# Remainder parts of MLP weights: every second half piece by an accumulating DMA, conversions three half pieces ahead

## The chip, the cores and the metric

The kernel runs on one core of a Trainium2 chip. The metric is device time in microseconds of one execution. The kernel before takes 2416.2 us (median of 2 runs, 2415.84 to 2416.57).

## The reference, cut to what matters

A decoder trunk of two layers for 256 tokens of width 2048, in float32. Each layer has a token mixer and then an MLP, both behind an RMSNorm and added to the residual stream. The mixer of layer 0 is latent attention (MLA), that of layer 1 a Mamba-2 scan (SSM).

```python
def squared_relu_mlp(h, w_in, w_out):
    u = jax.nn.relu(h @ w_in)
    return (u * u) @ w_out

for i in range(DEPTH):
    h = rms_norm(x, mix_norm_g[i])
    x = x + (mla_mixer(h, ...) if i % 2 == 0 else ssm_mixer(h, ...))
    h = rms_norm(x, mlp_norm_g[i])
    x = x + squared_relu_mlp(h, mlp_w_in[i], mlp_w_out[i])
```

`w_in` is [2048, 8192] and `w_out` is [8192, 2048], so each MLP reads 128 MB of float32 weights, and both of them 256 MB of the 452 MB that the whole kernel moves.

## The kernel before, in words

**Products.** The tokens are the stationary operand (two tiles of 128), the weights stream through TensorE 512 columns at a time. A float32 product is taken as three passes over operands that are split into a rounded part H (type float32r) and the exact remainder L = raw - H: for each 128 rows of weights and each token tile `block` issues H.H (L227), H.L (L228) and L.H (L229), where the second factor is the weights'. So the weights' H is needed by the first matmul and their L by the second.

**Pieces and half pieces.** A weight piece is [128, 4 x 512] float32, 1 MB. `Flow` holds the list of all pieces in the order of use (`sequence`, which puts MLA first, then MLP 0, SSM, MLP 1). Each MLP has 64 pieces of `w_in` (keys "mi") and 64 of `w_out` (keys "mo"). A piece is converted in two half pieces of [128, 1024]. The second element of a half's record, `k`, is the first of its four row blocks: 0 in the first half of a piece, 2 in the second.

- `load` takes one of three raw buffers (`wr`) and puts a 1 MB DMA on SyncE's queue (L75). A buffer is free again when both halves of its piece have been converted.
- `convert` takes one buffer each of the pools `wh` and `wl` (three of 4 KB per partition in each), lets ScalarE copy the half piece into `wh` with rounding (L101) and VectorE subtract: `wl` = raw - `wh` (L102).
- `piece` hands the halves out. Before it hands out half `j` it asks for the load of pieces up to three ahead, and for the conversion of halves up to `j + 2` (`ahead` is (3, 2)).

With three buffers, half `j + 2` goes into the buffers that half `j - 1` leaves. ScalarE's copy for `j + 2` therefore waits until TensorE has finished half `j - 1`, and there are then two half pieces of TensorE time before `j + 2` is wanted.

**Order.** The order on TensorE is that of the program text. A planner with costs of its own orders the instructions of the other engines and of the DMA queues, and sets all waits. Each engine and each queue takes its instructions in that order: an instruction that waits holds up those behind it.

**In the MLP.** A `w_in` block (four pieces) ends in a Relu (L384) and a Square (L385) on ScalarE for each token tile. Then come four transposes on TensorE and a split (L203 on ScalarE, L204 on VectorE), again for each tile. A `w_out` block (four pieces) ends in an addition to the residual on VectorE (L307). After four blocks of the one kind come four of the other, four times in each MLP. GpSimd has nothing to do in the MLP but three small instructions of the norm between two parts (L194, L299, L300).

**Gain rows.** `gain_tile` (L272) loads rows of gains, 256 KB each, on SyncE's queue into the pool `gb` of three buffers. They are read at the ends of MLA, MLP 0 and SSM (L284), and in the SSM at L914 and L948.

Of the kernel before, what the change touches and what calls it, by code (L numbers as in the profile page):

```python
"""MLA / Mamba-2 decoder trunk (2 layers, 256 tokens) for one NeuronCore.

Layout: tokens are the stationary operand of every large product (two tiles of
128), the weights stream through as the moving operand, 512 columns at a time.
Large float32 products run as three float32r passes over operands split into a
rounded part H and the exact remainder L (H.H + H.L + L.H).
RMSNorm's per-token factor is applied where a product leaves PSUM.  The scan has
one chunk of 256 tokens that starts from the zero state, so its output is the
intra-chunk term.
"""  # L10
# [2 lines left out]

# [10 lines left out]
AF = mybir.ActivationFunctionType  # L24
ALU = mybir.AluOpType
AX = mybir.AxisListType
PSUM = bass.MemoryType.PSUM
# [29 lines left out]


class Flow:
    """Weight pieces in the order of use: loaded, split into H and L, handed out."""  # L60

    def __init__(self, nc, pools, seq, ahead):
        self.nc, self.pools, self.seq, self.ahead = nc, pools, seq, ahead
# [17 lines left out]
    def convert(self, upto):  # L81
        while self.done < min(upto, len(self.halves)):
            j = self.done
            i, k, nk, n = self.halves[j]
            self.load(i + 1)
            raw = self.raw[i][:, k * n:(k + nk) * n]
            h = self.pools["wh"].tile([P, 1024], F32R, tag="wh", name=f"wh{j}")
            lo = self.pools["wl"].tile([P, 1024], F32R, tag="wl", name=f"wl{j}")
            if n == 64:
                for q, t in enumerate((h, lo)):  # L90
                    v = t.rearrange("p (k r n) -> p k r n", r=2, n=64)
                    w = raw.rearrange("p (k n) -> p k n", n=64)[:, 8 * q:8 * q + 8]
                    self.nc.scalar.activation(v[:, :, 0], w, AF.Copy)
                    self.nc.vector.tensor_tensor(v[:, :, 1], w, v[:, :, 0].bitcast(F32), ALU.subtract)
                self.split[j] = (h, lo)
                self.done += 1
                continue
            w = 512 if j == 0 else nk * n
            for o in range(0, nk * n, w):
                v = slice(o, o + w)  # L100
                self.last = self.nc.scalar.activation(h[:, v], raw[:, v], AF.Copy)  # L101
                self.nc.vector.tensor_tensor(lo[:, v], raw[:, v], h[:, v].bitcast(F32), ALU.subtract)  # L102
            self.split[j] = (h, lo)
            self.done += 1

    def piece(self, key):
        """Yields (first k tile, H, L) with H, L as [128, k tiles, columns]."""
        i = self.seq_at
        assert self.seq[i][0] == key, (self.seq[i][0], key)
        self.seq_at += 1  # L110
        while self.used < len(self.halves) and self.halves[self.used][0] == i:
            j = self.used
            self.load(i + self.ahead[0])
            self.convert(j + 1 + self.ahead[1])
            _, k, nk, n = self.halves[j]
            h, lo = self.split.pop(j)
            if n == 64:
                self.used += 1
                yield [t.rearrange("p (k n) -> p k n", n=P) for t in (h, lo)]
                return  # L120
            yield (k, nk, h[:, :nk * n].rearrange("p (k n) -> p k n", k=nk),
                   lo[:, :nk * n].rearrange("p (k n) -> p k n", k=nk))
            self.used += 1
# [4 lines left out]
class Trunk:  # L128
    def __init__(self, tc, ctx, d, out):
        self.tc, self.nc, self.d, self.out = tc, tc.nc, d, out  # L130
        nc = self.nc
        pool = lambda name, bufs, **kw: ctx.enter_context(tc.tile_pool(name=name, bufs=bufs, **kw))
        self.c = pool("const", 1)
        self.st = pool("stat", 24)
        self.res = pool("res", 1)
        self.xtp = pool("xt", 8)
        self.k4 = pool("k4", 8)
        self.s2 = pool("s2", 8)
        self.gb = pool("gb", 3)
        self.wp = {"raw": pool("raw", 3), "wh": pool("wh", 3), "wl": pool("wl", 3)}  # L140
        self.acc = pool("acc", 4, space=PSUM)
        self.sm = pool("sm", 2, space=PSUM)
        self.yp = pool("yp", 2, space=PSUM)
        self.queue, self.pump = [], None
        self.nsm = 0
        self.uid = 0

# [1 line left out]
    def name(self, s):  # L149
        self.uid += 1  # L150
        return f"{s}_{self.uid}"
# [35 lines left out]
        return pool.tile([P, 4, 256], dt, tag=pool.name, name=self.name(pool.name))  # L187

    def rsqrt(self, ssq, n, width, eps=EPS, scale=None):
        """(ssq / width + eps) ** -0.5, per token"""  # L190
        nc = self.nc
        v, r = self.stat(n), self.stat(n)
        nc.vector.tensor_scalar(v, ssq, 1.0 / width, eps, ALU.mult, ALU.add)  # L193
        nc.gpsimd.tensor_tensor(r, v, self.mhalf[:, :n], ALU.pow)  # L194
        return r
# [8 lines left out]
        self.nc.vector.tensor_tensor(lo, src, h.bitcast(F32), ALU.subtract)  # L204

    def transposes(self, src, h, lo, t, wide=True):
        """src [128 tokens, 512] -> H, L [128, 4, tokens of tile t]"""
        b = self.bank(wide)
        for j in range(4):
            self.nc.tensor.transpose(b[:, j * P:(j + 1) * P], src[:, j * P:(j + 1) * P], self.ident)  # L210
        sl = slice(t * P, (t + 1) * P)
        self.split_out(h[:, :, sl], lo[:, :, sl], b.rearrange("p (k n) -> p k n", k=4))

# [1 line left out]
    def block(self, keys, lhs, n=512, accs=None, first=True, last=True):  # L215
        nc = self.nc
        if accs is None:
# [14 lines left out]
        return accs  # L232

    def narrow_block(self, key, tiles, then):
        """64 columns: [H | L] of the weights is stationary, the tokens stream; the
        sum of both parts is taken by the product that brings tokens onto partitions"""
        nc = self.nc
        (w,) = self.flow.piece(key)
        acc = self.bank(False)
        for kt in range(16):  # L240
            for i in range(2):
                nc.tensor.matmul(acc[:, :256], w[kt // 8][:, kt % 8], tiles[kt // 4][i][:, kt % 4],
                                 start=kt == 0 and i == 0, stop=kt == 15 and i == 1)
        s = self.scratch()
# [16 lines left out]
            return h[:, (kt + off) % 4, sl], lo[:, (kt + off) % 4, sl]  # L261
        return lhs

# [1 line left out]
    def boundary_begin(self, gain):  # L265
        self.nx = [None] * 4
        self.nx_ssq = self.stat(8)
# [18 lines left out]
            self.later(0, lambda t=t, xg=xg: self.transposes(xg, h, lo, t, wide))  # L286

    def boundary_end(self):
        """to be called once every block is emitted; sets xT and its rstd"""
        self.xT = self.nx  # L290
        self.set_rstd(self.nx_ssq)

# [13 lines left out]
            x = self.x[t][nb]  # L306
            self.nc.vector.tensor_tensor(x, accs[t], x, ALU.add)  # L307

# [1 line left out]
    def start(self, seq):  # L310
        nc, d = self.nc, self.d
        self.flow = Flow(nc, self.wp, seq, (3, 2))
        cst = self.c.tile([P, C_END], F32, name="cst")
        self.cst = cst
        self.ident = cst[:, C_ID:C_ID + P]
# [51 lines left out]
        for n, at in enumerate(X_AT):  # L367
            self.later(at, lambda n=n: stats(n))

# [1 line left out]
    def mlp(self, layer, gain):  # L371
        nc = self.nc
        xT = self.xT
# [26 lines left out]
        if gain is not None:  # L400
            self.boundary_end()

# [1 line left out]
    def rope_tables(self, mp):  # L404
        nc = self.nc
        self.cc = mp.tile([P, 4, 64], F32, name="cc")
# [56 lines left out]
            nc.gpsimd.tensor_scalar(sv[:, :, 0:32], sn3, -1.0, None, ALU.mult)  # L463

    def rope(self, mp, x):
        """x [128, 2 token tiles, m, 64] in place"""
        nc = self.nc
        m = x.shape[2]
        cc, ss = (v.rearrange("p (t h) f -> p t h f", t=2)[:, :, 0:m] for v in (self.cc, self.ss))
# [5 lines left out]
        nc.gpsimd.tensor_tensor(x, a, b, ALU.add)  # L475

    def latent(self, accs, gain, tiles):
        """RMSNorm of a latent that still lacks its rstd, then its transposes"""
        nc = self.nc
        ssq = self.stat(2)  # L480
        for t in range(2):
# [227 lines left out]
            self.finalize(nb, self.block(wo(nb, range(4)), lhs))  # L709
        self.boundary_end()  # L710

# [1 line left out]
    def ssm(self, gain):  # L713
        with ExitStack() as ctx:
            sp = ctx.enter_context(self.tc.tile_pool(name="ssm", bufs=1, reuse_waits="tile"))
# [3 lines left out]
    def ssm_body(self, sp, dp, gain):  # L719
# [23 lines left out]
        self.later(0, setup)  # L743

        def conv(ev, ct, dst, lag, after):
            """causal depthwise conv and 2*silu, feature major; ev: 2 x [128 tokens, 512]"""
            def half(j):
                b = self.bank(early[0])
                for k in range(2):
# [38 lines left out]
        def dt_chain(b):  # L788
# [29 lines left out]
            def back():  # L818
# [2 lines left out]
                    nc.tensor.transpose(b[:, t * 64:(t + 1) * 64], cum[:, t * P:(t + 1) * P], self.ident[:64, :64])  # L821
                nc.tensor.matmul(b[:, 128:192], tri[:, P:256], la[:, 0], start=True, stop=True)
                nc.vector.tensor_scalar(ncum.rearrange("p t h -> p (t h)"), b[:, 0:128], -1.0, None, ALU.mult)
                # edge[:, 0]: decay of the tokens of tile 0 up to its end, times dt; edge[:, 1]: twice that from there on
                for t in range(2):
                    nc.vector.tensor_tensor(edge[:, t], b[:, 128:192], ncum[:, t], ALU.add)
                nc.scalar.activation(edge[:, 0], edge[:, 0], AF.Exp)
# [60 lines left out]
                        break  # L888

        def head(g, i, dg):  # L890
            """decay within the token tiles for one head; its product follows later"""
            h = 8 * g + i
            cm = sp.tile([P, S], F32, tag="cm", name=f"cm{h}", bufs=4)
            nc.sync.dma_start(cm, cumD[h:h + 1].to_broadcast([P, S]))
# [166 lines left out]


def pieces(w, n=512):
    """[K, N] -> [K / 512, N / n, 128, 4 * n], each piece one contiguous load"""
    K, N = w.shape
    return np.ascontiguousarray(w.reshape(K // 512, 4, P, N // n, n).transpose(0, 3, 2, 1, 4)).reshape(K // 512, N // n, P, 4 * n)

# [3 lines left out]


def rows(v, n):
    """[m * n] -> [m, 128, n], the same on every partition"""
    return np.ascontiguousarray(np.broadcast_to(v.reshape(-1, 1, n), (v.size // n, P, n)))


# [47 lines left out]
```

## Time and profile before

| | |
|---|---|
| median of 2 runs | 2416.2 us |
| profiled execution: span of its trace, the only time on record for it | 2417.7 us |
| TensorE (PE) busy | 2400.6 us |
| VectorE (DVE) busy | 1427.5 us |
| ScalarE (ACT) busy | 1189.8 us |
| GpSimd (POOL) busy | 131.2 us |
| DMA: moved, mean rate | 451.87 MB, 187 GB/s |
| granted TensorE clock, mean | 0.999 |

Times are from one profiled execution. PE is TensorE's matmuls and PEld its weight loads, SPq is SyncE's DMA queue. In a list of groups a row names the line, the engine, the operation, the buffers written and read (by the program's names), the shapes and the count, and then the busy time, the mean time of one in ns, and the idle time of the engine just before them with what ended it. In a list of waits a row has who waited for whom, the total in us, the number of waits and the longest. In a timeline a row has the start and the duration in us; the idle time before it and its releaser are in brackets. A row of a table of windows gives the busy time of each engine in that stretch, the granted clock, the mean busy share of the 16 DMA engines and the rate in GB/s.

### The profile page before, as it was taken

How to read it: one execution, taken by the hardware profiler on the slowest of the kernel's cores; microseconds unless marked ns; L12 is line 12 of the kernel's file. 1: busy time of each engine (PE TensorE's matmuls, PEld its weight loads, DVE VectorE, ACT ScalarE, POOL GpSimd, SP SyncE). 2: the span in 40 equal slices, each digit the busy share in tenths (PEclk: the TensorE clock that was granted, in tenths of full speed). 3: DMA queues.
4: the chain of work that ended last, by engine and by line, in shares of the span. 5: the costliest groups of instructions: out<-in, count | busy, mean ns of one | idle time of the engine just before them, and what ended most of it. 6: DMA issues, size and time to landing. Idle time of an engine off the chain costs nothing.

```text
span 2417.7 us, 28550 instructions
## 1 busy us (share of the span) xinstructions
PE 2400.6 (99%) x11136; PEld 1993.8 (82%) x11136; DVE 1427.5 (59%) x1911; ACT 1189.8 (49%) x1671; POOL 131.2 (5%) x136
## 2 busy tenths in 40 slices
PE   8999999999999999999999999999999999999999
PEld 6888888888888888888888888888888888888887
DVE  6675644545544545577789768666545454455444
ACT  6664444354354354455555455444553443443443
POOL 1330000000000000000022001110000000000000
PEclk9999999999999999999999999999999999999999
DMA  7333555555555555565456655555555555555554
GB/s 283 133 121 118 206 184 184 195 187 190 192 191 189 194 186 184 196 203 186 168 187 208 204 187 194 191 186 193 182 191 192 192 180 196 185 189 193 190 194 155
DMA packets 76679, 451.87 MB, mean 187 GB/s; under 512 B 8640, under 2 KB 17280, under 8 KB 25472
## 3 DMA queue, kind: packets, MB, share of 16 engines
q1 hardware_dynamic: 76464, 449.99, 54.3%
q8 instruction: 87, 1.43, 0.2%
q14 instruction: 48, 0.39, 0.0%
q10 hardware_dynamic: 80, 0.07, 0.0%
HBM read 447.86 MB, written 2.16 MB: 186 GB/s over the span
## 4 chain that ended last, share of the span: by engine, by line
PE 96%; DVE 2%; issue 1%; POOL 0%; ACT 0%; DMA 0%; SPq 0%; ACTq 0%; POOLq 0%; DVEq 0%
PE acc L227 30%; PE acc L229 30%; PE acc L228 30%; PE sm L210 1%; PE y L910 1%; PE yp L210 1%; DVE wl L102 0%; DMA wr<-ain 0%; PE sm L752 0%; PE yp L618 0%; PE sm L618 0%; ACT wh L101 0%; PE sm L616 0%; PE yp L616 0%; PE sm L874 0%
## 5 line engine op out<-in xcount | busy, mean ns | idle before, releaser
L102 DVE TENSOR_TENSOR wl<-wr,wh 128x1024 fp32r<-128x1024 f32 (+2 forms) x817 | 1003.7, 1230 | 890.5 <-ACT wh L101 889.2
L101 ACT ACTIVATE wh<-wr 128x1024 fp32r<-128x1024 f32 (+2 forms) x817 | 861.5, 1055 | 1057.4 <-PE acc L229 1024.3
L227 PE MATMUL acc<-wh,xt 128*128 128x512 f32 x1728 | 682.5, 395 | 5.9 <-ACT wh L101 5.9
L228 PE MATMUL acc<-wl,xt 128*128 128x512 f32 x1728 | 674.5, 390 | 1.6 <-DVE wl L102 1.6
L229 PE MATMUL acc<-wh,xt 128*128 128x512 f32 x1728 | 675.1, 391 | 0.0
L227 PE MATMUL acc<-wh,k 128*128 128x512 f32 x1408 | 551.9, 392 | 0.0
L229 PE MATMUL acc<-wh,k 128*128 128x512 f32 x1408 | 548.4, 389 | 0.0
L228 PE MATMUL acc<-wl,k 128*128 128x512 f32 x1408 | 547.9, 389 | 0.0
L227 PEld LDWEIGHTS acc<-wh,xt 128*128 128x128 f32 x1728 | 325.6, 188 | 71.2 <-ACT wh L101 6.3
L228 PEld LDWEIGHTS acc<-wl,xt 128*128 128x128 f32 x1728 | 325.7, 188 | 68.3 <-DVE wl L102 3.0
L229 PEld LDWEIGHTS acc<-wh,xt 128*128 128x128 f32 x1728 | 325.2, 188 | 68.8
L229 PEld LDWEIGHTS acc<-wh,k 128*128 128x128 f32 x1408 | 264.2, 188 | 55.4
L228 PEld LDWEIGHTS acc<-wl,k 128*128 128x128 f32 x1408 | 264.5, 188 | 54.1 <-DVE wl L102 0.4
L227 PEld LDWEIGHTS acc<-wh,k 128*128 128x128 f32 x1408 | 264.4, 188 | 53.8 <-issue 0.3
L194 POOL TENSOR_TENSOR st<-st,mhalf 128x4 f32<-128x4 f32 (+1 forms) x30 | 26.1, 871 | 1010.4 <-DVE st L193 1010.3
L384 ACT ACTIVATE s<-acc,rs 128x512 f32<-128x512 f32 x64 | 43.5, 680 | 31.5 <-PE acc L229 31.5
L761 DVE SCALAR_TENSOR_TENSOR s<-sm,cst,s 128x255 f32<-128x255 f32 (+2 forms) x114 | 54.6, 479 | 2.8 <-ACT s L758 1.3
L898 DVE TENSOR_SCALAR mt<-cm,ncum 128x128 f32<-128x128 f32 x128 | 45.8, 398 | 7.3 <-PE y L910 7.3
L307 DVE TENSOR_TENSOR x<-acc,x 128x512 f32<-128x512 f32 x72 | 46.1, 682 | 0.0
L899 ACT ACTIVATE mt<-mt 128x256 f32<-128x256 f32 x64 | 26.1, 412 | 40.0 <-DVE mt L898 40.0
L901 DVE SCALAR_TENSOR_TENSOR mt<-mt,dt,cb 128x128 f32<-128x128 f32 x128 | 40.6, 359 | 1.6 <-ACT mt L899 1.5
L910 PEld LDWEIGHTS y<-xtm,mt 128*128 128x128 f32 x256 | 35.3, 190 | 6.5 <-issue 3.8
(236 smaller groups left out, 1319.2 us busy)
## 6 DMA issues: line engine op xcount, KB each, us to landing
wr<-mi SPq DMA_DIRECT2D x128, 1024.0 KB, 4.8
wr<-mo SPq DMA_DIRECT2D x128, 1024.0 KB, 4.8
wr<-si SPq DMA_DIRECT2D x80, 1024.0 KB, 4.8
wr<-so SPq DMA_DIRECT2D x32, 1024.0 KB, 4.8
wr<-wo SPq DMA_DIRECT2D x16, 1024.0 KB, 4.8
wr<-ukv SPq DMA_DIRECT2D x8, 1024.0 KB, 4.8
cm<-cumD SPq DMA_DIRECT2D x64, 128.0 KB, 3.1
wr<-ain SPq DMA_DIRECT2D x7, 1024.0 KB, 8.9
```

The lines of the kernel that those rows point to most:

```text
L101: self.last = self.nc.scalar.activation(h[:, v], raw[:, v], AF.Copy)
L102: self.nc.vector.tensor_tensor(lo[:, v], raw[:, v], h[:, v].bitcast(F32), ALU.subtract)
L210: self.nc.tensor.transpose(b[:, j * P:(j + 1) * P], src[:, j * P:(j + 1) * P], self.ident)
L227: nc.tensor.matmul(accs[t][:, :n], ah, wh[:, q, :], start=st, stop=False)
L228: nc.tensor.matmul(accs[t][:, :n], ah, wl[:, q, :], start=False, stop=False)
L229: nc.tensor.matmul(accs[t][:, :n], al, wh[:, q, :], start=False, stop=en)
L307: self.nc.vector.tensor_tensor(x, accs[t], x, ALU.add)
L384: nc.scalar.activation(r, accs[t], AF.Relu, scale=rs[t])
L761: nc.vector.scalar_tensor_tensor(o[:, m:256], s[:, 0:256 - m], wc(i), o[:, m:256], ALU.mult, ALU.add)
L898: nc.vector.tensor_scalar(half(t), cm[:, t * P:(t + 1) * P], ncum[:, t, h:h + 1], 0.0, ALU.add, ALU.min)
L901: nc.vector.scalar_tensor_tensor(half(t), half(t), dt[:, t, h:h + 1], cb[g][:, 256 * t:256 * t + P], ALU.mult, ALU.mult)
L910: nc.tensor.matmul(y[t][:, o], half(t), xg[g][t][:, o], start=True, stop=True)
```

## The change

In the second half of each "mi" and "mo" piece, ScalarE writes `wh` as before. It then writes the negated rounded copy into `wl` as well (a second instruction with scale -1), and a DMA on GpSimd's queue adds the raw half piece to `wl` in place. VectorE does not touch that half. First halves, and all pieces of MLA and SSM, are converted as before. The pools `wh` and `wl` have four buffers each, the gain pool two in place of three, and conversions are asked for three half pieces ahead.

```diff
@@ Flow.convert
             w = 512 if j == 0 else nk * n
-            for o in range(0, nk * n, w):
+            if self.seq[i][0][0] in ("mi", "mo") and k:
+                self.last = self.nc.scalar.activation(h[:, :nk * n], raw, AF.Copy)
+                self.nc.scalar.activation(lo[:, :nk * n], raw, AF.Copy, scale=-1.0)
+                self.nc.gpsimd.dma_start(lo[:, :nk * n], raw, accum_op=ALU.add)
+                w = nk * n + 1
+            for o in range(0, nk * n, w) if w <= nk * n else ():
                 v = slice(o, o + w)
                 self.last = self.nc.scalar.activation(h[:, v], raw[:, v], AF.Copy)
                 self.nc.vector.tensor_tensor(lo[:, v], raw[:, v], h[:, v].bitcast(F32), ALU.subtract)
@@ Trunk.__init__
-        self.gb = pool("gb", 3)
-        self.wp = {"raw": pool("raw", 3), "wh": pool("wh", 3), "wl": pool("wl", 3)}
+        self.gb = pool("gb", 2)
+        self.wp = {"raw": pool("raw", 3), "wh": pool("wh", 4), "wl": pool("wl", 4)}
@@ Trunk.start
-        self.flow = Flow(nc, self.wp, seq, (3, 2))
+        self.flow = Flow(nc, self.wp, seq, (3, 3))
```

The rest of the diff takes out docstrings and comments.

## The prediction

> **What bounds the kernel now.** First the page: the busy times, then the chain that ended last.
>
> ```profile
> span 2417.7 us, 28550 instructions
> PE 2400.6 (99%) x11136; PEld 1993.8 (82%) x11136; DVE 1427.5 (59%) x1911; ACT 1189.8 (49%) x1671; POOL 131.2 (5%) x136
> PE 96%; DVE 2%; issue 1%; POOL 0%; ACT 0%; DMA 0%; SPq 0%; ACTq 0%; POOLq 0%; DVEq 0%
> ```
>
> TensorE is busy for all but 17.1 us of the span, and 96% of the chain is its matmuls. Busy is not proof of speed, so the next view cuts the span by stage (MLP 0 is the second row, MLP 1 the last; the table runs: us, PE, PEld, DVE, ACT, POOL, clock, DMA share, GB/s).
>
> ```profile
> 0.00:279.90 279.90, 269.36 (x1324) 223.90 (x1325) 183.83 (x410) 163.94 (x428) 52.14 (x71) 0.99 0.48 170
> 279.90:990.00 710.10, 710.10 (x3216) 589.65 (x3214) 358.25 (x335) 330.39 (x371) 1.78 (x3) 1.00 0.55 190
> 990.00:1700.00 710.00, 707.96 (x3382) 588.51 (x3381) 530.13 (x839) 370.48 (x515) 76.23 (x59) 1.00 0.57 192
> 1700.00:2417.70 717.70, 713.22 (x3220) 591.74 (x3218) 355.25 (x329) 325.04 (x358) 1.07 (x3) 1.00 0.55 186
> ```
>
> In MLP 0 TensorE has no gap at all, at full clock, while VectorE is busy for half the time. So in the stage that the change touches no engine is waited for by TensorE. The list of waits says the same from the other side.
>
> ```profile
> ACT wh L101 <- PE acc L229: 1024.3, 651, 4.8
> DVE wl L102 <- ACT wh L101: 889.2, 666, 2.7
> PE acc L227 <- ACT wh L101: 5.9, 1, 5.9
> PE sm L860 <- ACT wh L101: 1.6, 2, 0.8
> PE acc L228 <- DVE wl L102: 1.6, 3, 0.7
> SPq L75 <- DVE wl L102: 1946.5, 394, 11.4
> ```
>
> The converters wait for TensorE to free a buffer, 651 times; TensorE waits for a conversion 9.1 us in all (5.9 + 1.6 + 1.6). And the weight loads wait almost always for VectorE, which is the last to read a raw buffer. The timelines of ScalarE and VectorE in MLP 0 give the beat:
>
> ```profile
> 577.50 1.06 ACT L101 ACTIVATE wh<-wr 128x1024 fp32r<-128x1024 f32 x1 [1.66 <-PE acc L229]
> 580.22 1.06 ACT L101 ACTIVATE wh<-wr 128x1024 fp32r<-128x1024 f32 x1 [1.66 <-PE acc L229]
> 578.59 1.23 DVE L102 TENSOR_TENSOR wl<-wr,wh 128x1024 fp32r<-128x1024 f32 x1 [1.50 <-ACT wh L101]
> ```
>
> A half piece takes TensorE 2.72 us (580.22 - 577.50), a piece 5.44, and the 256 MLP pieces 1393 us. A conversion is done 2.32 us after its buffer is free (578.59 + 1.23 - 577.50).
>
> **The change part by part.** *What is removed.* 256 subtractions (128 pieces in each MLP, one half of each):
>
> ```profile
> L102 DVE TENSOR_TENSOR wl<-wr,wh 128x1024 fp32r<-128x1024 f32 (+2 forms) x817 | 1003.7, 1230 | 890.5 <-ACT wh L101 889.2
> L101 ACT ACTIVATE wh<-wr 128x1024 fp32r<-128x1024 f32 (+2 forms) x817 | 861.5, 1055 | 1057.4 <-PE acc L229 1024.3
> ```
>
> 256 x 1.23 = 315 us of VectorE. None of it is on the path: worth 0.
>
> *What is added on ScalarE.* 256 copies of 1.06 us, 271 us. Its load in an MLP rises from 330/710 by 1.06/5.44 to 66%: no bound by itself, cost 0 while the queue is on time. It is not on time where a `w_in` block ends:
>
> ```profile
> 565.03 0.69 ACT L384 ACTIVATE s<-acc,rs 128x512 f32<-128x512 f32 x1 [0.98 <-PE acc L229]
> 565.75 0.63 ACT L385 ACTIVATE s<-s 128x512 f32<-128x512 f32 x1
> 566.29 0.67 ACT L384 ACTIVATE s<-acc,rs 128x512 f32<-128x512 f32 x1
> 566.86 1.05 ACT L101 ACTIVATE wh<-wr 128x1024 fp32r<-128x1024 f32 x1
> 568.43 1.07 ACT L101 ACTIVATE wh<-wr 128x1024 fp32r<-128x1024 f32 x1
> ```
>
> By the beat the copy at 566.86 was due at 565.71 (568.43 - 2.72): 1.15 us late behind the block's Relu and Square. There are 32 such blocks (4 x 4 in each MLP), so 37 us are at stake if the new conversion has no slack.
>
> *What is added on the DMA side: the term that decides.* The wait moves from VectorE to a DMA that waits for ScalarE. I count L, from the moment that half j begins on TensorE (and half j-1 has freed its buffers) to the moment when the remainder of half j+3 is there. Three beats are available, plus the 0.22 us by which the first use of the remainder (L228) comes behind that of H:
>
> ```profile
> 2409.66 0.39 PE L227 MATMUL acc<-wh,k 128*128 128x512 f32 x1
> 2409.88 0.39 PE L228 MATMUL acc<-wl,k 128*128 128x512 f32 x1
> ```
>
> So L may be 3 x 2.72 + 0.22 = 8.38 us. Against it stand two copies on ScalarE (2.12), the issue on GpSimd, and the transfer to its landing. The trace has no DMA on GpSimd's queue, none that adds, and none from SBUF to SBUF. The nearest rows, for issue and landing:
>
> ```profile
> L75 SPq DMA_DIRECT2D wr<-mi x128: 327/328/328, 279.9 to 2302.3; - x128
> L472 POOL TENSOR_TENSOR ra<-qn,cc 128x256 f32<-128x256 f32 x8 | 15.1, 1884 | 15.1 <-DVE qn L558 15.0
> wr<-mi SPq DMA_DIRECT2D x128, 1024.0 KB, 4.8
> wr<-sidt SPq DMA_DIRECT2D x1, 512.0 KB, 3.4
> cm<-cumD SPq DMA_DIRECT2D x64, 128.0 KB, 3.1
> gb<-dsk SPq DMA_DIRECT2D x8, 256.0 KB, 2.6
> ```
>
> Issue: from 0.33 (SyncE's) to 1.88 us (the longest mean of a GpSimd instruction); I take 1.0, in the middle, as GpSimd's instructions are mostly nearer to that end. Transfer of 512 KB: as a plain copy 3.4 us. An addition in place has to fetch the raw half and the old `wl`, 1 MB of reads, which by the 1 MB row is 4.8 us. From these two rows a transfer has 2.0 us fixed and 1.4 us for each 512 KB. If its pieces are as small as those of the `cm` rows (1 KB per partition, 128 KB in 3.1, so 1.1 us beside the fixed 2.0), 1 MB of reads is 2.0 + 8 x 1.1 = 10.8 us. That is the upper end; 3.4 is the lower. I take 4.8: the add needs both operands, and its rows of 4 KB per partition are nearer to the 8 KB of a weight load than to 1 KB. [...]
>
> Alone on the engines, L = 2.12 + 1.0 + 4.8 = 7.92: it would just fit in 8.38. But it is not alone. The share of the DMA engines in MLP 0 is 0.55 (table above) for the loads alone, 1 MB in 5.44 us. Another 1 MB of reads adds 0.55: 1.10 of what there is, so 5.98 us per piece. And the two meet in time: a raw buffer is now released by the landing of the accumulating DMA, so the next load starts 8 us into the beat count, where the next accumulating DMA starts 0.6 us later (5.44 + 2.12 + 1.0 = 8.56). With both in flight for their whole length the transfer grows by 2.8, to L = 10.7.
>
> What a late remainder costs: second half of piece n+1 may not start before the start of piece n plus L - 0.22, and piece n+2 follows 2.72 later. Two periods are L + 2.50, so a period is 5.98 at L = 9.46 and 6.60 at L = 10.7. Over 5.44 that is 0.54 or 1.16 us, times 256: 138 or 297 us. I take the lower, at which the DMA engines would already be full all the time, and add the 37 us of the block ends, for which no slack is left.
>
> *Longer waits.* Behind the waiting DMA on GpSimd's queue stand only the three norm instructions (1.78 us of GpSimd in all of MLP 0), whose result is wanted a block later: 0. On SyncE, behind a load that waits for an accumulating DMA, stand other loads and the gain rows of the block ends; the load wait is in L already. On ScalarE nothing waits for the DMA.
>
> *Conversions further ahead, fourth buffers.* In MLA and SSM this can save at most the 9.1 us of waits above, most of which are the first weights (5.9, one wait): I take 0, at best -3.
>
> *Two gain buffers.* SyncE's queue in the SSM:
>
> ```profile
> 1216.16 0.33 SPq L272 DMA_DIRECT2D gb<-dsk  x1
> 1234.08 0.33 SPq L272 DMA_DIRECT2D gb<-sng  x1
> 1250.32 0.33 SPq L272 DMA_DIRECT2D gb<-dsk  x1
> 1285.17 0.33 SPq L272 DMA_DIRECT2D gb<-sng  x1
> ```
>
> Gain rows go in as buffers come free, a group or more before their use: the `dsk` row loaded at 1216 frees its buffer for the next only near 1285. With one buffer fewer a row comes some 16 to 35 us later and still in time; 0, at worst one 2.6 us landing for each of the eight groups, 20 us.
>
> **Sum**, against the profiled execution: 2417.7 + 138 + 37 = 2593; that execution stands 1.5 us above the median of the runs, so 2591 us, +7.2%.
>
> **The rivals.**
> *Hidden transfer (not slower).* The addition goes at the price of a copy: L = 2.12 + 1.0 + 3.4 = 6.5, or 7.9 with a load beside it (+1.4), below 8.38; the DMA share is 0.55 + 0.275 = 0.83. Then only block ends lose, (7.9 + 1.15 - 8.38) x 32 = 22 us at most, and the saving elsewhere is at most the 17.1 us that TensorE is idle at all: 2405 to 2440, likeliest 2420. It decides at L = 8.38. For it, the page's slices:
>
> ```profile
> DMA  7333555555555555565456655555555555555554
> GB/s 283 133 121 118 206 184 184 195 187 190 192 191 189 194 186 184 196 203 186 168 187 208 204 187 194 191 186 193 182 191 192 192 180 196 185 189 193 190 194 155
> ```
>
> In the first slice 283 GB/s take a share of 0.7 to 0.8, in the MLP 190 take 0.55: a fuller engine carries somewhat more per share, so 1.10 may overstate. Against it: two operands have to be read.
> *Slow addition.* Small pieces as in the `cm` row: L = 2.12 + 1.0 + 10.8 = 13.9, period 8.2, +2.76 x 256 = 707 us, 3120 us; half way from 4.8 to it (7.8) L is 10.9 before any sharing, and the time about 2730. For it: nothing in the trace shows what an add in the DMA engines costs. Against it: the long rows.
> *Faster by over 2%* would need 48 us, and TensorE has 17.1 us of idle time.
> That the change does not do what it says would be a planner that puts the copies for second halves behind other work on ScalarE; it shows as the block-end term, grown.
>
> **How the numbers follow.** Two-read transfer, 2465 to 2750 us: 0.46. Hidden, up to 2464: 0.28. Slow, above 2750: 0.25. Faster by over 2%: 0.01. A change of 2% (48 us) is about what a measurement of this kernel can tell from none. So slower 0.71, same 0.28, faster 0.01. The likeliest case's own range is 2500 to 2720. The range that is to hold 8 in 10 takes in the hidden case and the lower part of the slow one: 2410 to 2900; above it lies some 0.15, below it 0.03.
>
> **What would show it.** Right: in the MLP windows TensorE falls to about 90% busy, it waits at L228 for a DMA into `wl` some 250 times, the DMA share nears 1, ScalarE's copies no longer start every 2.72 us, and the landing of the adding DMA is 5 to 8 us; MLA and SSM keep their lengths. Wrong: landing near 3.5 us and a full TensorE (hidden), or landing of 10 us and more with TensorE at 70% (slow). Where the DMA is quick but its issue holds GpSimd for several us, the step on the issue failed.

## The result, and the profile after

The changed kernel takes 2547.97 us (median of 2 runs, 2545.12 to 2550.82) against 2416.2 us: a ratio of 1.0541, 95% interval 1.0524 to 1.0558. It is slower, as forecast, by 5.4% where the sum gave 7.2%. The profiled execution took 2545.1 us, with a span of 2543.2 us, 125.5 us more than before.

In the changed kernel's numbering the three matmuls of a block are L232 (H.H), L233 (H.L) and L234 (L.H). In the new branch L100 is the rounded copy, L101 the negated one and L102 the adding DMA; the old pair is now L106 and L107. The page first: busy times, then the chain that ended last, by engine and by line.

```profile
PE 2433.7 (96%) x11136; PEld 1994.2 (78%) x11136; DVE 1122.8 (44%) x1655; ACT 1427.1 (56%) x1927; POOL 355.4 (14%) x392
PE 62%; DMA 28%; issue 4%; ACT 4%; DVE 2%; POOL 1%; SPq 0%; POOLq 0%; ACTq 0%; DVEq 0%
DMA wl<-wr 28%; PE acc L233 20%; PE acc L234 18%; PE acc L232 18%; ACT wl L101 3%; PE y L915 1%; PE sm L215 1%; DVE wl L107 1%; DMA wr<-ain 0%; PE yp L215 0%; PE sm L757 0%; PE yp L623 0%; PE sm L623 0%; PE sm L621 0%; PE yp L621 0%
```

Before, 96% of the chain was matmuls. Now 28% of it lies in one transfer, `wl<-wr`, the adding DMA. VectorE lost 305 us of work (1427.5 - 1122.8), and none of that came back as time. The span by stage (same columns as in the prediction):

```profile
279.90:1055.00 775.10, 727.86 (x3199) 591.04 (x3198) 206.76 (x208) 445.18 (x497) 110.89 (x129) 0.99 0.94 257
1055.00:1765.00 710.00, 707.89 (x3387) 588.64 (x3386) 525.71 (x835) 374.08 (x516) 78.97 (x62) 1.00 0.58 195
1765.00:2543.20 778.20, 728.01 (x3210) 589.36 (x3208) 199.93 (x199) 440.26 (x484) 111.45 (x130) 1.00 0.94 257
```

MLP 0 went from 710.1 to 775.1 us, MLP 1 from 717.7 to 778.2: together the whole 125.5 us. The SSM has its 710.0 us as before. The DMA share in the MLP went from 0.55 to 0.94. Who waits, from the list of waits (SyncE's queue in the last row):

```profile
PEld acc L233 <- DMA wl<-wr: 127.1, 83, 3.6
PE acc L233 <- DMA wl<-wr: 92.5, 75, 3.2
POOL wl L102 <- ACT wl L101: 1375.1, 238, 93.2
ACT wh L106 <- DMA wr<-mo: 65.7, 39, 3.3
ACT wh L106 <- DMA wr<-mi: 50.0, 31, 2.9
SPq L75 <- DMA wl<-wr: 1422.4, 253, 9.8
```

TensorE waits at L233, the matmul that reads the remainder, and nowhere else in an MLP. It waits 75 times and not 256: two adds in three are on time. The third column of the DMA queues below is a share of 16 engines over the span; the issues give the median time to landing.

```profile
q1 hardware_dynamic: 76464, 449.99, 50.5%
q0 software_dynamic: 36864, 134.23, 28.3%
wr<-mi SPq DMA_DIRECT2D x128, 1024.0 KB, 6.0
wl<-wr POOLq DMA_DIRECT2D x256, 512.0 KB, 6.2
```

By the time of its packets one add occupies every DMA engine for 0.283 x 2543.2 / 256 = 2.81 us. A load of 1 MB takes 0.505 x 2543.2 x 1.049 / 450 = 2.99 us. Together that is 5.80 us of engine time for a piece that TensorE works off in 5.44.

### The profile page after: what moved, and what is told of

Same layout as the page of the kernel before. It is cut to its first block, busy times and chain, and to the rows that moved or that the text cites. A ratio compares the mean times of both kernels' runs of the same rounds, so it can differ in the third digit from the quotient of the medians.

```text
span 2543.2 us, 29542 instructions
## 1 busy us (share of the span) xinstructions
PE 2433.7 (96%) x11136; PEld 1994.2 (78%) x11136; DVE 1122.8 (44%) x1655; ACT 1427.1 (56%) x1927; POOL 355.4 (14%) x392
## 3 DMA queue, kind: packets, MB, share of 16 engines
q0 software_dynamic: 36864, 134.23, 28.3%
## 4 chain that ended last, share of the span: by engine, by line
PE 62%; DMA 28%; issue 4%; ACT 4%; DVE 2%; POOL 1%; SPq 0%; POOLq 0%; ACTq 0%; DVEq 0%
DMA wl<-wr 28%; PE acc L233 20%; PE acc L234 18%; PE acc L232 18%; ACT wl L101 3%; PE y L915 1%; PE sm L215 1%; DVE wl L107 1%; DMA wr<-ain 0%; PE yp L215 0%; PE sm L757 0%; PE yp L623 0%; PE sm L623 0%; PE sm L621 0%; PE yp L621 0%
## 5 line engine op out<-in xcount | busy, mean ns | idle before, releaser
L107 DVE TENSOR_TENSOR wl<-wr,wh 128x1024 fp32r<-128x1024 f32 (+2 forms) x561 | 691.6, 1236 | 1248.6 <-ACT wh L106 1247.6
L106 ACT ACTIVATE wh<-wr 128x1024 fp32r<-128x1024 f32 (+2 forms) x561 | 590.3, 1054 | 581.0 <-PE acc L234 411.1
L233 PE MATMUL acc<-wl,xt 128*128 128x512 f32 x1728 | 681.3, 394 | 37.9 <-DMA wl<-wr 36.1
L232 PE MATMUL acc<-wh,xt 128*128 128x512 f32 x1728 | 685.1, 396 | 5.8 <-ACT wh L106 5.8
L234 PE MATMUL acc<-wh,xt 128*128 128x512 f32 x1728 | 677.7, 392 | 0.0
L233 PE MATMUL acc<-wl,k 128*128 128x512 f32 x1408 | 555.4, 394 | 56.4 <-DMA wl<-wr 56.3
L232 PE MATMUL acc<-wh,k 128*128 128x512 f32 x1408 | 554.0, 393 | 0.0
L234 PE MATMUL acc<-wh,k 128*128 128x512 f32 x1408 | 550.7, 391 | 0.0
L101 ACT ACTIVATE wl<-wr 128x1024 fp32r<-128x1024 f32 x256 | 271.6, 1061 | 346.7 <-PE acc L233 346.5
L102 POOL DMA_DIRECT2D wl<-wr x256 | 221.2, 864 | 1469.0 <-ACT wl L101 1375.1
L233 PEld LDWEIGHTS acc<-wl,xt 128*128 128x128 f32 x1728 | 326.9, 189 | 118.9 <-DMA wl<-wr 51.6
L232 PEld LDWEIGHTS acc<-wh,xt 128*128 128x128 f32 x1728 | 326.9, 189 | 72.1 <-ACT wh L106 6.4
L234 PEld LDWEIGHTS acc<-wh,xt 128*128 128x128 f32 x1728 | 326.9, 189 | 68.5
L233 PEld LDWEIGHTS acc<-wl,k 128*128 128x128 f32 x1408 | 265.6, 189 | 128.4 <-DMA wl<-wr 75.5
L232 PEld LDWEIGHTS acc<-wh,k 128*128 128x128 f32 x1408 | 265.6, 189 | 54.9 <-issue 0.3
L234 PEld LDWEIGHTS acc<-wh,k 128*128 128x128 f32 x1408 | 265.5, 189 | 54.5
L100 ACT ACTIVATE wh<-wr 128x1024 fp32r<-128x1024 f32 x256 | 268.2, 1048 | 0.0
L947 POOL TENSOR_TENSOR xtm<-s,xtm 128x512 f32<-128x512 f32 x16 | 24.3, 1539 | 176.7 <-DVE s L937 176.7
```

The lines of the kernel that those rows point to most:

```text
L100: self.last = self.nc.scalar.activation(h[:, :nk * n], raw, AF.Copy)
L101: self.nc.scalar.activation(lo[:, :nk * n], raw, AF.Copy, scale=-1.0)
L102: self.nc.gpsimd.dma_start(lo[:, :nk * n], raw, accum_op=ALU.add)
L232: nc.tensor.matmul(accs[t][:, :n], ah, wh[:, q, :], start=st, stop=False)
L233: nc.tensor.matmul(accs[t][:, :n], ah, wl[:, q, :], start=False, stop=False)
L234: nc.tensor.matmul(accs[t][:, :n], al, wh[:, q, :], start=False, stop=en)
```

## The experiments

Two theories stood against each other. By **theory 1** the DMA engines' time is short, because an add costs as much as two reads. By **theory 2** the chain of ScalarE's copy, GpSimd's issue and the fixed part of a landing is too long for a lead of three half pieces. A third candidate was ScalarE itself, which the prediction charged with 37 us at the block ends. The edits are against the changed kernel if nothing else is said. Where no number of runs is given, the time is that of one run. Beside these runs the kernel before had medians of 2417.2 to 2417.9 us.

### Lead and pools without the DMA

```diff
-            if self.seq[i][0][0] in ("mi", "mo") and k:
+            if False:
```

> Every half piece is converted by ScalarE and VectorE as before; only the pools (four wh, four wl, two gain buffers) and the three half pieces of lead are those of the changed kernel. All theories that put the loss on the accumulating DMA expect 2408 to 2418 us: TensorE waited 9.1 us for conversions before, of which 5.9 us are the first weights. If the lead or the two gain buffers cost something of their own, it is above 2425 us.

Measured: 2415.18 us (11 runs, 2414.35 to 2416.2), ratio to before 0.9991, interval 0.9982 to 1.0. The fourth buffers, the longer lead and the two gain buffers cost nothing, and give at most 0.2%. The loss is the new branch's.

### ScalarE's extra copies without the DMA

```diff
-                self.nc.gpsimd.dma_start(lo[:, :nk * n], raw, accum_op=ALU.add)
+                self.nc.vector.tensor_tensor(lo[:, :nk * n], raw, h[:, :nk * n].bitcast(F32), ALU.subtract)
```

> ScalarE writes the negated copy into wl as in the changed kernel, and VectorE then overwrites it with the remainder; there is no DMA on GpSimd's queue. This prices ScalarE's 256 extra copies by themselves. Theory 1 expects 2412 to 2422 us. If ScalarE's lateness at block ends was worth 37 us, as the prediction's sum has it, it is 2440 to 2455 us.

Measured: 2415.05 us (10 runs, 2414.15 to 2415.99), ratio 0.9991, interval 0.9981 to 1.0001. So 256 extra copies on ScalarE, with the block ends among them, cost nothing where VectorE makes the remainder. The prediction's 37 us are not there as a cost of their own.

### A copy in place of the add

```diff
-                self.nc.gpsimd.dma_start(lo[:, :nk * n], raw, accum_op=ALU.add)
+                self.nc.gpsimd.dma_start(lo[:, :nk * n].bitcast(F32), raw)
```

> The DMA on GpSimd's queue copies the raw half piece over wl instead of adding it, so the remainder of these halves is left out and wl holds the raw weights; every instruction, wait and byte count stays. Theory 1 (the DMA engines' time: an add costs two reads) expects about 2425 us, 2416 to 2445: a 4 KB packet of a copy takes 159 ns in the trace of before against 328 ns for an adding one, the engines' work falls from 8 x (370 + 349) ns = 5.75 us per piece to about 4.3 us of the 5.44. Theory 2 (the chain of fixed steps is too long for the lead: ScalarE's copies, GpSimd's issue, the fixed part of a landing) expects stalls to stay where ScalarE is late: above 2460 us.

Measured: 2422.28 us. The same queue and bytes cost 5 us instead of 130. The queue, the issues and a window of MLP 0 in this run:

```profile
q0 software_dynamic: 36864, 134.23, 14.6%
wl<-wr POOLq DMA_DIRECT2D x256, 512.0 KB, 4.8
400.00:900.00 500.00, 499.89 (x2240) 412.79 (x2239) 136.58 (x135) 308.77 (x334) 47.52 (x90) 1.00 0.81 284
```

The engines move 284 GB/s here while TensorE stays full, more than the 258 of the changed kernel in the same window: the counted bytes are not the limit. But the chain is shorter too. GpSimd's issue takes 0.53 us in place of 0.86, and the quickest landing 2.8 us in place of 4.5. So this run prices the add against a copy, and does not by itself decide between the two theories.

A copy occupies the engines for 0.146 x 2420.4 / 256 = 1.38 us, the add for 2.81: a factor of 2.04 for equal bytes. By packet, tallied from the traces (load and add in the changed kernel, copy in this run; ns of one packet):

```
                               median   mean
8 KB, load from HBM            309      370
4 KB, copy on GpSimd's queue   159      171
4 KB, add on GpSimd's queue    328      349
```

### Half of the load

```diff
+            if self.seq[self.loaded][0][0] in ("mi", "mo"):
+                self.nc.sync.dma_start(t[:, 1024:2048], src[:, 1024:2048])
...
-            raw = self.raw[i][:, k * n:(k + nk) * n]
+            raw = self.raw[i][:, (2 if self.seq[i][0][0] in ("mi", "mo") else k) * n:][:, :nk * n]
```

> Loads of MLP pieces bring only the second half (512 KB), and both halves are converted from it, so half of the MLP weights are left out; all conversions and the adding DMAs stay. Theory 1 expects about 2425 us, 2416 to 2445, with the adding DMA landing in about 4.5 to 5 us: the engines need 8 x (185 + 349) ns = 4.3 us per piece. Theory 2 expects no change of the chain ahead of the add, and a time above 2500 us.

Measured: 2445.14 us, at the upper edge of theory 1 and far from theory 2. Most of the loss goes with 0.5 MB of loads per piece, though ScalarE, GpSimd and the add itself are as they were. But some 28 us of it stay, and TensorE still waits 24 times for an add, while the engines have a fifth of their time free (a window in MLP 0):

```profile
400.00:900.00 500.00, 494.55 (x2198) 403.98 (x2197) 137.07 (x133) 300.84 (x325) 75.88 (x88) 1.00 0.82 187
```

So theory 1 is not all of it.

### A longer lead

```diff
-        self.s2 = pool("s2", 8)
+        self.s2 = pool("s2", 5)
-        self.wp = {"raw": pool("raw", 3), "wh": pool("wh", 4), "wl": pool("wl", 4)}
+        self.wp = {"raw": pool("raw", 3), "wh": pool("wh", 5), "wl": pool("wl", 5)}
-        self.flow = Flow(nc, self.wp, seq, (3, 3))
+        self.flow = Flow(nc, self.wp, seq, (3, 4))
```

The SSM's `cm` and `mt` pools also lose a buffer each.

> Five wh and five wl buffers and a lead of four half pieces; to make room the scratch pool has five buffers in place of eight, cm three and mt five, which touches the SSM, so the MLP stages are what is compared (775 and 778 us in the changed kernel, 710 and 718 before). Theory 1 (the DMA engines' time) expects them to stay near their throughput bound, 750 to 780 us each. Theory 2 (too little lead for the chain) expects them back at 710 to 725 us each.

Measured: 2500.94 us. From their first to their last weight matmul, MLP 0 takes 757 us and MLP 1 751, against 782 and 773 in the changed kernel and 714 and 711 before: inside the range of theory 1, but shorter than without the longer lead. One half piece more of lead takes back 47 us of the 132. The same 500 us of MLP 0, this run first and the changed kernel second:

```profile
400.00:900.00 500.00, 480.11 (x2106) 387.32 (x2105) 129.56 (x126) 279.90 (x308) 73.31 (x85) 1.00 0.99 266
```

```profile
400.00:900.00 500.00, 467.00 (x2032) 378.64 (x2032) 125.38 (x122) 276.13 (x294) 70.72 (x82) 0.99 0.95 258
```

With the longer lead the DMA share is 0.99 against 0.95: the chain now keeps the engines nearly full. A landing is even later here (median 7.6 us against 6.2), and hurts less, since it has 2.72 us more to land in. The loads come late as well:

```profile
ACT wh L106 <- DMA wr<-mo: 317.9, 117, 8.4
ACT wh L106 <- DMA wr<-mi: 232.2, 104, 7.2
```

ScalarE waits 550 us for them in this run, against 116 in the changed kernel. A raw buffer still comes free only when an add has landed, and there are three. Whether a fourth one would help at this lead was not run.

### Both relieved

The last two edits together.

> Half loads (the first half of each MLP piece is left out, both halves are converted from the second) together with five wh and wl buffers and four half pieces of lead. Half loads alone left 26 us of stalls, the longer lead alone about 82 us. If the loss has just these two causes, engine time and cover, nothing is left with both relieved: TensorE full in the MLP, 2416 to 2430 us, the rest of it from the smaller SSM pools. If something else of the adding DMA costs time, it stays above 2435 us.

Measured: 2415.68 us. TensorE has no gap left in the window, though all 256 adds run, and the MLPs are back at 714 and 711 us:

```profile
400.00:900.00 500.00, 500.00 (x2248) 414.87 (x2247) 138.74 (x134) 311.33 (x336) 78.36 (x91) 1.00 0.84 190
```

So the two causes together hold the whole loss. With equal pools and a lead of four, whole loads cost 2498.8 - 2413.6 = 85 us of span: the engines' time, with the late loads that go with it (ScalarE's waits for weight loads of the MLPs are 41 us here, against 550). The step back to a lead of three costs the other 44 us (2543.2 - 2498.8): that is cover. Taken in the other order, half loads give 100 us (2543.2 - 2443.2) and the lead 30 (2443.2 - 2413.6). The two causes overlap, and the split depends on which is relieved first. The smaller SSM pools cost nothing.

### More raw buffers

```diff
-        self.wp = {"raw": pool("raw", 3), "wh": pool("wh", 4), "wl": pool("wl", 4)}
+        self.wp = {"raw": pool("raw", 4), "wh": pool("wh", 4), "wl": pool("wl", 4)}
-        self.flow = Flow(nc, self.wp, seq, (3, 3))
+        self.flow = Flow(nc, self.wp, seq, (4, 3))
```

The scratch pool `s2` and the SSM's `cm` and `mt` pools are as small as in the run with the longer lead.

> Four raw buffers and loads four pieces ahead, the same smaller SSM pools, everything else as in the changed kernel. ScalarE waited 116 us for loads in the changed kernel. If these late loads (a raw buffer comes free only when the add has landed) are what makes the conversions late, the MLP stages fall to 715 to 735 us each. If theory 1 holds they stay at 765 to 780 us each.

Measured: 2549.84 us, no change from 2547.97. ScalarE's waits for weight loads of the MLPs are gone from the list of waits, so with a lead of three they were not on the path.

### Half of the adds

```diff
-            if self.seq[i][0][0] in ("mi", "mo") and k:
+            if self.seq[i][0][0] in ("mi", "mo") and k and i % 2:
```

> Only the second halves of every second MLP piece go by the adding DMA, the others by VectorE: 128 adds in place of 256. Theory 1 expects about 2425 us, 2416 to 2440: the engines need on average 8 x 370 + 4 x 349 ns = 4.4 us per piece of 5.44. Theory 2, by which each add is late on its own, expects half of the loss: about 2480 us.

Measured: 2417.1 us, no loss. Theory 2's proportional 2480 is out: an add is not late by itself. In the same window as above the share of the engines is 0.78 and TensorE is full:

```profile
400.00:900.00 500.00, 500.00 (x2250) 414.98 (x2249) 193.58 (x180) 269.08 (x290) 38.71 (x45) 1.00 0.78 237
```

### Twice the adds

```diff
-            if self.seq[i][0][0] in ("mi", "mo") and k:
+            if self.seq[i][0][0] in ("mi", "mo"):
```

> Both halves of every MLP piece go by the adding DMA: 512 adds. Theory 1 (the DMA engines' time) expects 8 x 370 + 16 x 349 ns = 8.5 us of each engine per piece, so at least 8.5 us for a piece of 5.44: 2416 + 256 x 3.1 = 3200 us or more, up to 3400 where the engines idle as well, with a DMA share of 0.9 to 1. Theory 2 (only the chain's length against the lead) expects a half piece every L / 3 with L near 9 us, 3.0 us against 2.72: about 2560 us.

Measured: 3021.68 us. The kind of bound is theory 1's, and 2560 us is out; the size is off. A piece takes 5.44 + (3019.9 - 2413.6) / 256 = 7.81 us where the sum of packet times gave 8.5. The reason for part of that stands in a window of MLP 0:

```profile
400.00:1000.00 600.00, 476.01 (x1896) 360.05 (x1894) 25.38 (x38) 327.89 (x357) 130.77 (x152) 0.95 1.04 266
```

The share of 1.04 means that packets overlap on an engine here, so packet times add up to more than the time they take. It also means that a share of 0.99 alone does not prove the engines full. Part of the 7.81 us may be the clock, which is 0.968 in this run.

### The adding DMA with the old lead

Three `wh`, three `wl` and three gain buffers, and a lead of (3, 2).

> The adding DMA with the buffers and the lead of before (three wh, three wl, three gain buffers, two half pieces ahead). A second half then has two half pieces of cover, 5.44 + 0.22 us, against at least 0.2 + 1.06 + 0.28 + 4.48 = 6.0 us for ScalarE's copy, the step to GpSimd and the quickest landing, 7.7 us at the median landing of 6.2. Period of a piece 6.0 to 7.7 us instead of 5.44 plus what is lost at block ends: both theories expect 2560 to 2980 us, likeliest 2750; theory 1 with the DMA share falling well below 0.94, since the engines then wait for the chain.

Measured: 2837.82 us, as both theories allowed. Here it is the chain that binds: in the stage's window the share is only 0.82. But up to 114 us of it are neither: the granted clock is down.

```profile
400.00:900.00 500.00, 426.07 (x1746) 336.59 (x1745) 108.39 (x106) 241.62 (x262) 59.51 (x69) 0.94 0.82 222
```

### Stalls without the DMA

Against the kernel before:

```diff
+            if self.seq[i][0][0] in ("mi", "mo") and k and i % 2:
+                for _ in range(2):
+                    self.nc.vector.tensor_tensor(lo[:, :nk * n], raw, h[:, :nk * n].bitcast(F32), ALU.subtract)
-        self.wp = {"raw": pool("raw", 3), "wh": pool("wh", 3), "wl": pool("wl", 3)}
+        self.wp = {"raw": pool("raw", 3), "wh": pool("wh", 2), "wl": pool("wl", 2)}
-        self.flow = Flow(nc, self.wp, seq, (3, 2))
+        self.flow = Flow(nc, self.wp, seq, (3, 1))
```

> The kernel before with two wh and two wl buffers, one half piece of lead, and VectorE's subtraction done three times over in the second half of every second MLP piece: TensorE is made to stall some 128 times for 2 to 3 us with no DMA on GpSimd's queue, about 2416 + 128 x 2.4 = 2720 us. The granted TensorE clock was 0.96 in the run with the adding DMA and the old lead, in dips to half speed of 3.4 us that each begin within about a microsecond of the end of a stall. If the dips follow TensorE's stalls, they appear here too, mean clock 0.95 to 0.985. If they come from the adding DMAs, the clock stays at 0.999.

Measured: 2936.98 us; the forecast of 2720 was 217 us short, of which the clock is up to 117 us. TensorE's waits for VectorE add up to 363 us (178 waits) where the forecast had 307. The mean granted clock:

```profile
core 0: 2935.2 us, clock 0.960
```

So the clock fell with TensorE's stalls without any adding DMA as well: 0.960, as in the run with the old lead, against 0.999 in the kernel before. No variant beats the kernel before by more than 0.2%.

## Why the prediction was right

**What bounds.** TensorE was full in the MLP (busy for 710.10 of the 710.10 us of MLP 0), so freeing VectorE could give nothing. Shown by the two runs in which VectorE has lost work and TensorE stays full: 2417.1 us with half of the adds, and 2415.7 us with all of them and both causes relieved.

**The price of the add.** The step "an addition in place has to fetch the raw half and the old `wl`", priced by the 1 MB row, was the author's estimate, as no row of before shows an add. It holds as a price: 2.81 us of engine time against a copy's 1.38, 2.04 times. That the second read is the reason is not visible in the trace, which counts 134.23 MB for the adds as for the copies. The hidden rival stood on the price of a copy; the copy run shows what it would have given, 2422 us, where the rival said 2420. The slow rival's 10.8 us never appeared in the changed kernel: the quickest landing was 4.5 us, the slowest 10.4. (Half way to that rival the prediction's formula gives about 2740 us, not 2730; nothing hangs on it.)

**The engines' time, oversized.** The term of 138 us came from 0.55 + 0.55 = 1.10, a period of 5.98. Measured with the longer lead it is 85 us, a period of 5.77, and that figure still holds the late loads. The add's own share is 2.76 us of 5.44 (0.283 x 2498.8 / 256 in the run with the longer lead), 0.51 and not 0.55. The packets make the difference: a mean of 349 ns for the 4 KB of an add against 380 ns for the 8 KB of a load before.

**The block ends, misplaced.** The 37 us "for which no slack is left" do not exist at that place: ScalarE's copies alone cost nothing. Of TensorE's 75 waits 43 are for pieces of `w_out`, whose blocks have no Relu and Square, and 57 are for the second or fourth piece of a block of either kind. Why those two are later than the others is open. In place of the 37 us stand 44 us of missing cover, which the prediction knew (the formula with L) but left at its lower end, because full engines seemed to include it. So the sum of 175 us was 130 us: in this split one term was 53 too large, and the other right in size by luck.

**The chain, one copy shorter.** The prediction put two copies (2.12 us) ahead of the issue. The planner put the negated copy first:

```profile
569.84 1.06 ACT L101 ACTIVATE wl<-wr 128x1024 fp32r<-128x1024 f32 x1 [1.43 <-PE acc L233]
570.80 1.04 ACT L100 ACTIVATE wh<-wr 128x1024 fp32r<-128x1024 f32 x1
572.78 1.06 ACT L106 ACTIVATE wh<-wr 128x1024 fp32r<-128x1024 f32 x1 [0.93 <-PE acc L234]
575.27 1.06 ACT L101 ACTIVATE wl<-wr 128x1024 fp32r<-128x1024 f32 x1 [1.43 <-PE acc L233]
```

It waits only for the last reader of `wl`, and so begins 0.23 us ahead of the beat: 575.27 - 572.78 = 2.49 instead of 2.72. One stretch of the chain in time (start, duration):

```profile
605.28 0.24 PE acc L233
605.54 1.07 ACT wl L101
606.61 0.28 issue
606.90 9.50 DMA wl<-wr
616.44 0.50 PE acc L233
```

Ahead of the issue pass 1.06 + 0.28 - 0.23 = 1.11 us, so an add has 8.38 - 1.11 = 7.27 us from issue to landing. In the trace 82 of the 256 adds take longer. The waits at L233 number 83 (weight loads) and 75 (matmuls), and 77 of the 83 are for one of those 82 adds. The expected "some 250" waits were too many, since lateness isn't shared evenly: the median landing of 6.2 us is in time, the tail is not.

GpSimd's issue, taken as 1.0 us, is 0.86:

```profile
L102 POOL DMA_DIRECT2D wl<-wr x256 | 221.2, 864 | 1469.0 <-ACT wl L101 1375.1
```

A landing is counted from the start of its issue, so the 0.86 us lie inside it. The prediction added its 1.0 us to a 4.8 us row that already held SyncE's 0.33. Its 5.8 us for issue and transfer alone on the engines compare with 4.5 us at the quickest.

**The rest of the 125.5 us.** The matmuls' waits are 92.5 us. Each wait counts from the end of the matmul before it, which ends 0.39 us after its start though without a wait the next starts after 0.23: 75 x 0.16 = 12 us. The clock, 0.995 after 0.999, is some 10 us. About 11 us are not assigned.

The prediction left out the clock altogether. In the changed kernel it is small; with longer stalls it would not have been.

## What to carry to other kernels

An adding DMA took 2.04 times a copy's time on the DMA engines here (2.81 against 1.38 us for 512 KB): before work is moved there, add twice its bytes to the share of the stage that it will run in, and see whether that passes 1 (here 0.55 + 0.55 = 1.10, and 85 us were lost even with the longer lead). Below it, the tail of the landings against the lead decided here, not the median: with half loads (shares of 0.82 and 0.84) a lead of three half pieces lost some 28 us and one of four nothing. Half of the adds cost nothing, all of them 5%. And where TensorE was full, taking 305 us off VectorE, busy for 59% of the span, gave nothing; it put a longer path in the work's place.

## What was not expected of the hardware

TensorE's granted clock dropped to half for 3.4 us, sometimes 6.8 us, in a stall or just behind it: seven times in the changed kernel, at stalls of 1.8 to 3.2 us. From the run with the old lead:

```profile
515.66 0.39 PE L232 MATMUL acc<-wh,k 128*128 128x512 f32 x1
519.52 0.79 PE L233 MATMUL acc<-wl,k 128*128 128x512 f32 x1 [3.47 <-DMA wl<-wr]
520.11 0.63 PE L234 MATMUL acc<-wh,k 128*128 128x512 f32 x1
520.53 0.63 PE L232 MATMUL acc<-wh,k 128*128 128x512 f32 x1
520.96 0.63 PE L233 MATMUL acc<-wl,k 128*128 128x512 f32 x1
```

This dip begins at 518.4 us, inside the stall, and lasts 6.8 us. After 3.47 us of idling the matmuls start every 0.43 us instead of 0.23. Half the time of the dips is the most that they can cost: up to 114 us for 53 dips in this run, 117 for 62 in the run with the stalls made by VectorE, 14 in the changed kernel and 3 in the kernel before. Of the idle gaps of 1.5 to 2 us some had a dip that began in them or within 2 us of their end (5 of 16 in the run with the old lead, 23 of 100 in that with VectorE's stalls), of those of 3 to 3.5 us most (23 of 31, and 17 of 17), of those below 1 us none in these two runs. The kernel before has one dip behind three gaps of 0.3 to 0.6 us, so short gaps in a row are not proved safe.
